# Keeping split weights in DRAM as halves, and moving subtractions and additions of squares to GpSimd

## The chip, the cores and the metric

The kernel runs on one core of a Trainium2 chip. The metric is the device time of one execution in microseconds, the median of three runs. A profile was taken of one further execution.

## The reference, cut to what matters

The program is a decoder trunk of two residual layers on one sequence of 2048 tokens with 1024 channels, all in float32.

```
xn = rms_norm(h, norm_g[layer])
even layer: z = xn @ w_in_even -> u, v, ga, xb, gb, qm, gm
  ya = chunked_sgu(u, v) * silu(ga)      # LayerNorm of v, 128x128 mixing inside chunks
  yb = multiscale_pool(xb) * silu(gb)    # trailing means of 2, 4, 8, 16 tokens, then a 128x128 map
  ym = memory_attention(qm, mem) * silu(gm)
  h  = h + concat(ya, yb, ym) @ w_out_even
odd layer: z = xn @ w_in_odd -> qc, kc, vc, gc, da, db, gd, qm, gm
  yc = swa_sink_attention(qc, kc, vc) * silu(gc)   # window of 128
  yd = conformer_conv(da, db) * silu(gd)           # 31 taps per channel, LayerNorm, swish, 512x512 map
  ym = memory_attention(qm, mem) * silu(gm)
  h  = h + concat(yc, yd, ym) @ w_out_odd
```

## The kernel before, in words

The tokens are cut into four blocks of 512 (`TB`), and each block passes through an even and an odd stage, eight stages in the order E0, E1, O0, E2, O1, E3, O2, O3 (`order`, line 921). In the trace the stages begin at about 0, 253, 453, 745, 955, 1210, 1433 and 1695 us.

**Matrix products in halves.** Every factor is split into a high half (a cast to the reduced type fp32r on ScalarE, `hi_of`, line 119) and a low half (the float32 value minus the high half, `lo_of`, line 122). A product is three matmuls (`mm3`, lines 126 to 128): high by high, high by low, low by high.

**Weights.** `wslot` (line 137) brings in one slot of 128 x 1024 floats (512 KB): one load into the buffer `wr` (two of these), the cast into `wh` on ScalarE, and the subtraction into `wl` on GpSimd or VectorE. There are four `wh` and four `wl`. In even stages each third subtraction goes to VectorE, in odd stages all go to GpSimd (`share`). An even stage uses 35 slots: 20 units of the input projection (`w_cm`), 10 of the output projection (`w_o`), 4 for v (`w_v`), and one half as large for the pool map (`bw`). An odd stage uses 38: 24, 10, 2 for keys and values (`w_kvc`) and 2 for the map behind the convolution (`dpw`). Eight more are used once for the memory (`wkv`). Each of the four blocks loads and splits its layer's slots anew.

**Work around the weights.** `proj` is one unit of input projection, 24 matmuls of 512 columns. `gate` turns a unit into a gate path. `finish` (line 330) splits a finished branch of 128 x 512 into `yh` and `yl`; there are ten of these in each stage. `out_steps` runs an output projection in eight steps, each of which ends with the addition of the result to a residual row on VectorE (line 521, `row`). `Norm` loads the next stage's input, squares it on ScalarE and adds up the squares on VectorE (`square_sum`, line 160, `p`); `split` (line 482) makes the next stage's input halves `xnh` and `xnl`, eight of each. `pace` ties the subtractions of `split`, three at a time, behind the row additions of a stage's last output projection.

**Order.** A planner in the compiler of the kernel orders each engine's instructions by a simulated timeline; the order is fixed before the run, so it changes when the engine of an instruction changes. All transfers are issued by SyncE's queue, in that order. In an odd stage the 31 taps of the convolution (line 689) are fed to VectorE two at a time after each projection (`pump`), and the events of the attention are written out by hand in `_SEQ`.

Of the kernel before, what the change touches and what calls it, by code (L numbers as in the profile page):

```python
# [10 lines left out]
F32 = mybir.dt.float32  # L11
F32R = mybir.dt.float32r
AF = mybir.ActivationFunctionType
ALU = mybir.AluOpType
# [4 lines left out]
P = 128  # L19
S = 2048  # L20
D = 1024
TB = 512
# [30 lines left out]
def trunk(ctx: ExitStack, tc: tile.TileContext, x, mem, par, par1, wkv, w_v, w_cm0, w_kvc, w_cm1, w_o0, w_o1, awt, bw, dpw, abse, out):  # L53
# [68 lines left out]
    def lo_of(eng, lo, raw, hi):  # L122
        eng.tensor_tensor(lo, raw, hi.bitcast(F32), op=ALU.subtract)  # L123
# [10 lines left out]

    turns, share = [0], [3]

    def wslot(src, n=1024, eng=None):
        raw = rp.tile([P, 1024], F32, tag="wr", name="wr", bufs=2)[:, :n]
        hi = wp.tile([P, 1024], F32R, tag="wh", name="wh", bufs=4)[:, :n]
        lo = wp.tile([P, 1024], F32R, tag="wl", name="wl", bufs=4)[:, :n]  # L140
        nc.sync.dma_start(raw, src)
        hi_of(hi, raw)
        turns[0] += 1
        lo_of(eng or (V if turns[0] % share[0] == 0 else G), lo, raw, hi)
        return hi, lo

    def view(pair, pat, **kw):
        return [t.rearrange(pat, **kw) for t in pair]
# [11 lines left out]
    def square_sum(srcs, n_buf=1):  # L160
        bufs = []
        for _ in range((n_buf + 2) // 2):
            t = p_tile().rearrange("p a b -> p (a b)")
            bufs += [t[:, :TB], t[:, TB:]]
        total, bufs = bufs[0], bufs[1:]
        for i, src in enumerate(srcs):
            sq = bufs[i % n_buf] if i else total
            A.activation(sq, src, AF.Square)
            if i:
                V.tensor_tensor(total, total, sq, op=ALU.add)  # L170
        return total, bufs[0]

    def token_scale(sums, width):
# [146 lines left out]
                bg.pop(0)()  # L320

    def proj(xn, w_cm, unit):
        wh, wl = view(wslot(w_cm[unit]), "p (k c) -> p k c", k=KC)
        pb = mm_bank()
        for k in range(KC):
            mm3(pb, wh[:, k, :], wl[:, k, :], xn[0][:, k, :], xn[1][:, k, :], k == 0, k == KC - 1)
        pump(2)
        return pb

    def finish(y):  # L330
        hi = half("yh", 4, F32R)
        lo = half("yl", 4, F32R)
        done[0] = hi_of(hi, y)
        lo_of(V, lo, y, hi)
        return hi, lo

    def gate(st, w_cm, unit):
# [113 lines left out]
    class Norm:  # L451
# [30 lines left out]
        def split(self):  # L482
            flush()
            xn = xn_tile()

            def one(k):
                hi_of(xn[0][:, k, :], self.xs[k])
                lo_of(V, xn[1][:, k, :], self.xs[k], xn[0][:, k, :])
            rate[0] = 3
            paced.extend(lambda k=k: one(k) for k in range(KC))  # L490
            return xn
# [12 lines left out]
    def out_steps(st, first, ys):  # L504
        rows = st["rows"]
        w_o = w_o1 if st["odd"] else w_o0
        n = len(ys)
        per = KC // n
        ws = {}

        def step(u):
            q, c = divmod(u, per)
            if q not in ws:
                ws[q] = view(wslot(w_o[first + q]), "p (u k n) -> p u k n", u=per, k=n)
            wh, wl = ws[q]
            pb = mm_bank()
            for k in range(n):
                mm3(pb, wh[:, c, k, :], wl[:, c, k, :], ys[k][0], ys[k][1], k == 0, k == n - 1)
            pump(2)
            row = rows[u // 2][:, (u % 2) * TB:(u % 2 + 1) * TB]  # L520
            add = V.tensor_tensor(row, pb, row, op=ALU.add)  # L521
            pace(add)

        return [lambda u=u: step(u) for u in range(KC)]
# [74 lines left out]
    def even(st, ahead):  # L599
        b, xn = st["b"], st["xn"]  # L600
        if b:
            t, wt, abias = sgu_tile()
            nc.sync.dma_start(t, sgu_d)
        xhs = [half("xc", 4) for _ in range(NT)]
        for hf in range(2):
            if b == 0 and hf == 0:
                ws = first_v
            else:
                with behind(ET.DVE):
                    ws = [view(wslot(w_v[hf, j]), "p (k n) -> p k n", k=4) for j in range(2)]  # L610
            for tt in range(NT):
                pb = mm_bank()[:, :256]
                ts = slice(tt * P, (tt + 1) * P)
                for k in range(KC):
                    wh, wl = ws[k // 4]
                    mm3(pb, xn[0][:, k, ts], xn[1][:, k, ts], wh[:, k % 4, :], wl[:, k % 4, :], k == 0, k == KC - 1)
                A.copy(xhs[tt][:, hf * 256:(hf + 1) * 256], pb)
                if hf:
                    standard(xhs[tt], xhs[tt])
        if b == 0:  # L620
            with behind(ET.PE, ET.SP, ET.Pool, ET.DVE, ET.Activation):
                wt, abias = prep_even()
                prep_odd()
            mx, total = mem_start()
            diag = token_scale(total, 256)
        q = queries(st, w_cm0, (16, 17), 4, "qm")
        if b == 0:
            memt = mem_norm(mx, diag)
        gm = [gate(st, w_cm0, 18 + n) for n in range(2)]
        if b == 0:  # L630
            prep_mem(memt)
        start_rows(st, x[b])
        hx = st["hx"] = sb.tile([P, 4, HALO + TB], F32, tag="hx", name="hx", bufs=1)
        V.tensor_copy(hx[:, :, :HALO], xtail)
        df = [None] * 4
        ym = memory(0, q, gm, lambda tt: pool_windows(st, df, tt))
        nx = ahead()
        wb = view(wslot(bw, TB), "p (g d) -> p g d", g=4)
        yb = [pool_map(st, g, df[g], wb) for g in range(3)]
        project_out(st, 8, ym)  # L640
        yb.append(pool_map(st, 3, df[3], wb))
        ya = [sgu(st, 0, xhs, wt, abias)]
        steps = out_steps(st, 4, yb)
        for f in steps[:4]:
            f()
        with behind(ET.PE):
            nx.measure()
        for f in steps[4:]:
            f()
        nx.scale()  # L650
        rate[0] = 4
        for n in range(1, 4):
            ya.append(sgu(st, n, xhs, wt, abias))
        st["next"] = nx.split()
        project_out(st, 0, ya)
        flush()
        store_rows(st, h1[b])
# [33 lines left out]

    def keys(st):
        xn, kt, va = st["xn"], st["kt"], st["va"]
        ws = [view(wslot(w_kvc[q]), "p (k n) -> p k n", k=4) for q in range(2)]
        for tt in range(NT):
            pb = mm_bank()
            ts = slice(tt * P, (tt + 1) * P)
            for k in range(KC):
                wh, wl = ws[k // 4]
                mm3(pb[:, :256], xn[0][:, k, ts], xn[1][:, k, ts], wh[:, k % 4, :], wl[:, k % 4, :],  # L700
                    k == 0, k == KC - 1)
            pump(2)
            ss = small("kss", 2)
            sq = short()
            for h in range(2):
                A.activation(sq[:, h * 64:h * 64 + 64], pb[:, h * 64:h * 64 + 64], AF.Square, accum_out=ss[:, h:h + 1])
            A.copy(va[:, 1 + tt, :], pb[:, P:2 * P])
            r = rsq("krs", ss, 2, 1.0 / 64)
            kn = sb.tile([P, P], F32, tag="kn", name="kn", bufs=2)
            for h in range(2):  # L710
                V.scalar_tensor_tensor(kn[:, h * 64:h * 64 + 64], pb[:, h * 64:h * 64 + 64], r[:, h:h + 1], gk,
                                       op0=ALU.mult, op1=ALU.mult)
            tb = tr_bank()
            T.transpose(tb[:, :P], kn, ident)
            stack_keys(kt[:, :, P + tt * P:P + (tt + 1) * P], tb[:, :P])
        V.tensor_copy(ktail, kt[:, :, TB:].bitcast(F32))
        V.tensor_copy(vtail, va[:, NT, :])
# [188 lines left out]
        return hd  # L906

    def conv_mix(st, hd, ys):
        ws = [view(wslot(dpw[q]), "p (k n) -> p k n", k=2) for q in range(2)]
        for u in range(4):  # L910
            pb = mm_bank()
            for k in range(4):
                us = slice(u * P, (u + 1) * P)
                wh, wl = ws[k // 2]
                mm3(pb, wh[:, k % 2, us], wl[:, k % 2, us], hd[k][0], hd[k][1], k == 0, k == 3)
            pace(V.scalar_tensor_tensor(ys[u], pb, 0.25, ys[u], op0=ALU.mult, op1=ALU.mult))
        return [finish(y) for y in ys]
# [3 lines left out]
    order = [(0, 0), (0, 1), (1, 0), (0, 2), (1, 1), (0, 3), (1, 2), (1, 3)][:_STAGES]  # L921
    lead = Norm(x[0], par_of("ng0"), False, 3)
    nc.sync.dma_start(pc, par)
    first_v = [wslot(w_v[0, 0], eng=G)]
    lead.measure()
    with behind(ET.DVE):
        first_v.append(wslot(w_v[0, 1], eng=V))
    first_v = [view(w, "p (k n) -> p k n", k=4) for w in first_v]
    xn = lead.scale_split()
    for n, (is_odd, b) in enumerate(order):  # L930
# [114 lines left out]
```

## Time and profile before

| what | value |
|---|---|
| median of three runs | 1969.15 us (1968.65 to 1969.47) |
| the profiled execution's own time | 1970.85 us |
| its span, from the first to the last instruction | 1968.9 us |
| busy in the span: TensorE, weight loads | 96%, 80% |
| busy in the span: VectorE, ScalarE, GpSimd | 70%, 42%, 44% |
| moved by transfers | 218.96 MB, 111 GB/s on average |

An engine's share says how much of the span it had an instruction in flight. Matmuls overlap each other, so 96% for TensorE says how little of the span it was without work, not that each instant was full. What a change can save is in the places where TensorE waits, and these are read from its idle times with what ended them.

### The profile page before, as it was taken

To read this page: it belongs to the slowest core of one execution; us is meant where nothing else is said; L and a number is where in the kernel's file an instruction comes from. 1 tells how busy PE (TensorE), PEld (TensorE's weight loads), DVE (VectorE), ACT (ScalarE), POOL (GpSimd) and SP (SyncE) were. 2 spreads that over 40 slices of the span, in tenths; PEclk is the share of its full clock that TensorE was granted. 3 is DMA by queue.
4 is the path that set the end of the run, shared out by engine and by line. 5 is a ranking of instruction groups with operands and counts; after the bars stand their busy time and mean duration, and the time that the engine had idled before them with its cause. 6 is when DMAs were issued, how large, how long until landed. Compare 5 with 4: busy or idle time off the path is not lost.

```text
span 1968.9 us, 26523 instructions
## 1 busy us (share of the span) xinstructions
PE 1899.1 (96%) x10034; PEld 1569.0 (80%) x10034; DVE 1374.2 (70%) x2262; ACT 825.3 (42%) x1663; POOL 872.8 (44%) x593
## 2 busy tenths in 40 slices
PE   6999999999998999999999899999999989999999
PEld 6878888787886878878788687988878767888687
DVE  6776544645999673565699967355569986699954
ACT  4453324423355442442435443353333544435532
POOL 3672225323555443623445443453245544445542
PEclk9999999999999999999999999999999999999999
DMA  5443353334322334232532233432252223532122
GB/s 207 152 137 113 102 173 106 109 99 166 97 86 70 103 107 160 96 113 86 177 97 67 68 124 132 136 113 97 86 178 86 75 66 111 166 108 71 59 76 75
DMA packets 61440, 218.96 MB, mean 111 GB/s; under 512 B 6785, under 2 KB 6913, under 8 KB 61185
## 3 DMA queue, kind: packets, MB, share of 16 engines
q1 hardware_dynamic: 61312, 217.27, 33.9%
q8 instruction: 79, 1.29, 0.3%
q14 instruction: 49, 0.39, 0.1%
HBM read 198.63 MB, written 18.61 MB: 110 GB/s over the span
## 4 chain that ended last, share of the span: by engine, by line
PE 47%; DVE 9%; ACT 1%; issue 0%; DMA 0%; POOL 0%; ACTq 0%; POOLq 0%; SPq 0%
PE mm L126 12%; PE mm L127 12%; PE mm L128 12%; DVE cv L689 3%; PE cv L128 2%; PE cv L126 2%; PE cv L127 2%; DVE xnl L123 1%; PE pv L417 1%; PE tr L385 1%; PE tr L312 1%; PE tr L313 1%; DVE row L521 1%; PE pv L357 1%; DVE pt L853 1%; DVE q L123 0%
## 5 line engine op out<-in xcount | busy, mean ns | idle before, releaser
L123 POOL TENSOR_TENSOR wl<-wr,wh 128x1024 fp32r<-128x1024 f32 (+1 forms) x250 | 606.6, 2428 | 866.6 <-ACT wh L120 808.2
L120 ACT CAST wh<-wr 128x1024 fp32r<-128x1024 f32 (+1 forms) x300 | 312.6, 1042 | 655.0 <-PE mm L127 358.6
L126 PE MATMUL mm<-xnh,wh 128*128 128x512 f32 x1176 | 464.3, 395 | 0.4 <-ACT u L354 0.4
L128 PE MATMUL mm<-xnh,wl 128*128 128x512 f32 x1176 | 461.6, 393 | 0.2 <-DVE wl L123 0.2
L127 PE MATMUL mm<-xnl,wh 128*128 128x512 f32 x1176 | 460.7, 392 | 0.0
L689 DVE SCALAR_TENSOR_TENSOR cv<-hx,dwh,cv 128x512 f32<-128x512 f32 x464 | 349.0, 752 | 9.1
L128 PEld LDWEIGHTS mm<-xnh,wl 128*128 128x128 f32 x1176 | 221.3, 188 | 47.2 <-issue 1.2
L127 PEld LDWEIGHTS mm<-xnl,wh 128*128 128x128 f32 x1176 | 221.6, 188 | 45.9 <-issue 2.8
L126 PEld LDWEIGHTS mm<-xnh,wh 128*128 128x128 f32 x1176 | 221.4, 188 | 44.0 <-issue 0.6
L126 PE MATMUL mm<-yh,wh 128*128 128x512 f32 x534 | 215.5, 406 | 23.8 <-DVE row L521 14.4
L127 PE MATMUL mm<-yl,wh 128*128 128x512 f32 x534 | 210.6, 394 | 1.1 <-DVE yl L123 1.1
L128 PE MATMUL mm<-yh,wl 128*128 128x512 f32 x534 | 210.5, 394 | 0.0
L521 DVE TENSOR_TENSOR row<-mm,row 128x512 f32<-128x512 f32 x160 | 109.1, 686 | 122.9 <-PE mm L128 122.6
L126 PEld LDWEIGHTS mm<-yh,wh 128*128 128x128 f32 x534 | 100.9, 190 | 56.3 <-DVE row L521 23.1
L127 PEld LDWEIGHTS mm<-yl,wh 128*128 128x128 f32 x534 | 101.0, 189 | 21.6 <-DVE yl L123 2.0
L128 PEld LDWEIGHTS mm<-yh,wl 128*128 128x128 f32 x534 | 100.9, 189 | 21.4 <-issue 0.2
L123 DVE TENSOR_TENSOR wl<-wr,wh 128x1024 fp32r<-128x1024 f32 (+1 forms) x50 | 66.3, 1326 | 68.8 <-ACT wh L120 68.7
L403 ACT ACTIVATE p<-tr,mnb,qm 128x256 f32<-128x256 f32 x128 | 70.6, 561 | 69.6 <-DVE mnb L400 65.1
L377 POOL TENSOR_SCALAR p<-p,mrd 128x256 f32<-128x256 f32 x128 | 64.1, 521 | 79.5 <-DVE mrd L406 78.4
L126 PE MATMUL mm<-wh,xnh 128*128 128x256 f32 x320 | 91.8, 287 | 2.9 <-ACT xnh L120 1.8
L128 PE MATMUL mm<-wh,xnl 128*128 128x256 f32 x320 | 91.0, 285 | 1.3 <-DVE xnl L123 1.1
L126 PE MATMUL cv<-xnh,wh 128*128 128x512 f32 x232 | 92.1, 397 | 0.0
(226 smaller groups left out, 3378.3 us busy)
## 6 DMA issues: line engine op xcount, KB each, us to landing
wr<-in_w_cm_dram SPq DMA_DIRECT2D x176, 512.0 KB, 3.5
wr<-in_w_o_dram SPq DMA_DIRECT2D x80, 512.0 KB, 3.5
wr<-in_w_v_dram SPq DMA_DIRECT2D x16, 512.0 KB, 3.5
row<-in_x_dram SPq DMA_DIRECT2D x16, 512.0 KB, 4.1
h<-row SPq DMA_DIRECT2D x16, 512.0 KB, 3.5
row<-h SPq DMA_DIRECT2D x16, 512.0 KB, 3.9
out_dram<-row SPq DMA_DIRECT2D x15, 512.0 KB, 2.7
x<-in_x_dram SPq DMA_DIRECT2D x8, 512.0 KB, 3.6
```

Of the source, the lines that this page charges most:

```text
L120: return A.copy(hi, raw)
L123: eng.tensor_tensor(lo, raw, hi.bitcast(F32), op=ALU.subtract)
L126: T.matmul(out, lhsT=lh, rhs=rh, start=first, stop=False)
L127: T.matmul(out, lhsT=lh, rhs=rl, start=False, stop=False)
L128: T.matmul(out, lhsT=ll, rhs=rh, start=False, stop=last)
L312: T.matmul(out, lhsT=q[g][:, cols], rhs=keys[:, g], start=True, stop=False)
L313: T.matmul(out, lhsT=q[g][:, cols], rhs=keys[:, 2 + g], start=False, stop=True)
L357: T.matmul(sp[:, 2 * tt:2 * tt + 2], lhsT=sq[:, tt * P:(tt + 1) * P], rhs=par_of("bones"), start=True, stop=True)
L377: G.tensor_scalar(p[:, h, :], p[:, h, :], rd[:, h:h + 1], 1.0, op0=ALU.mult, op1=ALU.mult)
L403: A.activation(p[:, h, :], banks[h // 2][:, (h % 2) * 256:(h % 2) * 256 + 256], AF.Exp, bias=nb[:, h:h + 1], scale=qr[:, tt, h:h + 1], acc ...
L521: add = V.tensor_tensor(row, pb, row, op=ALU.add)
L689: V.scalar_tensor_tensor(dst, src, w, acc, op0=ALU.mult, op1=ALU.add)
```

## The change

Three things change. A slot of weights is now one buffer of two halves (`w`, 128 x 2 x 1024, four of them, as many bytes as the four `wh` and four `wl`). At its first use it is loaded and split as before and then written to DRAM as halves (1 MB); at each later use the 1 MB of halves is loaded straight into the buffer, with no cast and no subtraction. The eight slots of the memory have no key and stay as they were. The low halves of the branches (`finish`) and of the next stage's input (`split`) are computed on GpSimd in place of VectorE. The additions of squares in `square_sum` go to GpSimd too, but for the very first norm, which has three buffers.

```diff
-    def wslot(src, n=1024, eng=None):
+    halves = {}
+
+    def wslot(src, n=1024, eng=None, key=None):
+        w = wp.tile([P, 2, 1024], F32R, tag="w", name="w", bufs=4)[:, :, :n]
+        hi, lo = w[:, 0], w[:, 1]
+        if key in halves:
+            nc.sync.dma_start(w.bitcast(F32), halves[key])
+            return hi, lo
         raw = rp.tile([P, 1024], F32, tag="wr", name="wr", bufs=2)[:, :n]
-        hi = wp.tile([P, 1024], F32R, tag="wh", name="wh", bufs=4)[:, :n]
-        lo = wp.tile([P, 1024], F32R, tag="wl", name="wl", bufs=4)[:, :n]
         nc.sync.dma_start(raw, src)
         hi_of(hi, raw)
         turns[0] += 1
         lo_of(eng or (V if turns[0] % share[0] == 0 else G), lo, raw, hi)
+        if key:
+            halves[key] = tc.dram_tile([P, 2, n], F32, name="w_" + "_".join(map(str, key)))
+            nc.sync.dma_start(halves[key], w.bitcast(F32))
         return hi, lo
...
             if i:
-                V.tensor_tensor(total, total, sq, op=ALU.add)
+                (V if n_buf > 1 else G).tensor_tensor(total, total, sq, op=ALU.add)
...
         done[0] = hi_of(hi, y)
-        lo_of(V, lo, y, hi)
+        lo_of(G, lo, y, hi)
...
                 hi_of(xn[0][:, k, :], self.xs[k])
-                lo_of(V, xn[1][:, k, :], self.xs[k], xn[0][:, k, :])
+                lo_of(G, xn[1][:, k, :], self.xs[k], xn[0][:, k, :])
```

Every call of `wslot` but that for `wkv` now passes a key that names its matrix and slot.

## Rows read from the trace of the kernel before

**Rows 1.** The page: span, and busy time of each engine.

```profile
span 1968.9 us, 26523 instructions
PE 1899.1 (96%) x10034; PEld 1569.0 (80%) x10034; DVE 1374.2 (70%) x2262; ACT 825.3 (42%) x1663; POOL 872.8 (44%) x593
```

**Rows 2.** What TensorE waited for: total us, times, longest us.

```profile
PE mm L126 <- DVE row L521: 15.7, 17, 1.6
PE tr L179 <- DVE p L170: 11.1, 1, 11.1
PE mm L126 <- ACT yh L120: 8.5, 4, 3.9
PE pv L862 <- DVE pt L853: 5.0, 3, 2.3
```

**Rows 3.** Timelines at a stage's end: start, us, what, [idle before <- releaser].

```profile
254.24 0.50 PE L126 MATMUL cv<-yh,wh 128*128 128x512 f32 x1 [1.52 <-DVE row L521]
...
945.95 4.09 DVE L123 TENSOR_TENSOR xnl<-x,xnh 128x512 fp32r<-128x512 f32 x3
949.96 0.68 DVE L521 TENSOR_TENSOR row<-mm,row 128x512 f32<-128x512 f32 x1
...
946.74 2.75 POOL L123 TENSOR_TENSOR wl<-wr,wh 128x1024 fp32r<-128x1024 f32 x1 [5.06 <-ACT wh L120]
...
1699.51 0.50 PE L126 MATMUL mm<-yh,wh 128*128 128x512 f32 x1 [1.00 <-DVE row L521]
```

**Rows 4.** Stretches of O1: us, busy us (instructions) of PE, PEld, DVE, ACT, POOL, PEclk, transfers.

```profile
985.00:995.00 10.00, 10.00 (x46) 8.29 (x45) 9.10 (x14) 3.22 (x5) 3.21 (x2) 1.00 0.37 107
...
1095.00:1105.00 10.00, 7.68 (x40) 5.45 (x39) 9.77 (x19) 6.97 (x21) 5.88 (x6) 1.00 0.16 52
1115.00:1125.00 10.00, 6.09 (x22) 4.66 (x19) 9.91 (x22) 7.14 (x21) 3.00 (x5) 0.66 0.17 53
```

**Rows 5.** Groups by line and shape: busy us, mean ns | idle before.

```profile
L123 POOL TENSOR_TENSOR wl<-wr,wh 128x1024 fp32r<-128x1024 f32 x248 | 604.0, 2437 | 857.5 <-ACT wh L120 799.1 <-PE mm L128 24.3 <-ACT pt L387 11.8
L120 ACT CAST wh<-wr 128x1024 fp32r<-128x1024 f32 x296 | 310.1, 1048 | 651.2 <-PE mm L127 358.6 <-issue 110.2 <-PE cv L127 66.7
L123 DVE TENSOR_TENSOR yl<-gt,yh 128x512 fp32r<-128x512 f32 x80 | 66.3, 845 | 12.3 <-ACT yh L120 12.3
L170 DVE TENSOR_TENSOR p<-p 128x512 f32<-128x512 f32 x59 | 54.0, 916 | 26.3 <-ACT p L168 25.0
L841 POOL TENSOR_TENSOR p<-p,crd 128x512 f32<-128x512 f32 x32 | 32.7, 1042 | 7.9 <-DVE crd L838 7.9
```

**Rows 6.** Durations ns min/median/max of single lines, first and last start.

```profile
L123 POOL TENSOR_TENSOR wl<-wr,wh x250: 1292/2402/3143, 11.1 to 1944.9; 128x1024 fp32r<-128x1024 f32 x123, 128x512 fp32r<-128x512 f32 x2
L123 DVE TENSOR_TENSOR yl<-gt,yh x80: 675/686/2546, 149.3 to 1944.3; 128x512 fp32r<-128x512 f32 x80
L123 DVE TENSOR_TENSOR xnl<-x,xnh x28: 674/685/2891, 249.5 to 1691.3; 128x512 fp32r<-128x512 f32 x28
L677 DVE COPY htail<-hx x16: 167/945/2060, 506.4 to 1826.8; 128x30 f32<-128x30 f32 x16
```

**Rows 7.** Transfers: a load of weights, a larger one, the busiest stretch.

```profile
wr<-in_w_cm_dram SPq DMA_DIRECT2D x176, 512.0 KB, 3.5
...
sgu<-sgu_d SPq DMA_DIRECT2D x3, 768.0 KB, 4.3
...
2.00:8.00 6.00, 0.00 (x0) 0.00 (x0) 2.15 (x4) 3.39 (x7) 0.00 (x0) 1.00 0.95 370
```

**Rows 8.** E0 and O0 by engine, as rows 4; last are transfer share, GB/s.

```profile
0.00:253.00 253.00, 234.47 (x1330) 197.67 (x1330) 163.97 (x233) 107.31 (x178) 116.11 (x86) 1.00 0.42 140
...
453.00:745.00 292.00, 280.94 (x1416) 227.99 (x1415) 233.35 (x407) 130.89 (x288) 131.25 (x87) 0.99 0.33 108
```

**Rows 9.** What ScalarE's squares waited for: total us, times, longest us.

```profile
ACT p L168 <- DMA x<-h: 16.4, 7, 3.8
...
ACT p L168 <- DMA x<-in_x_dram: 10.2, 6, 2.5
```

More of the change, by code (lines that the diff above doesn't have):

```diff
@@ L322, in proj @@
     def proj(xn, w_cm, unit):
-        wh, wl = view(wslot(w_cm[unit]), "p (k c) -> p k c", k=KC)
+        wh, wl = view(wslot(w_cm[unit], key=("cm", int(w_cm is w_cm1), unit)), "p (k c) -> p k c", k=KC)
         pb = mm_bank()
@@ L513, in step @@
             if q not in ws:
-                ws[q] = view(wslot(w_o[first + q]), "p (u k n) -> p u k n", u=per, k=n)
+                ws[q] = view(wslot(w_o[first + q], key=("o", int(st["odd"]), first + q)), "p (u k n) -> p u k n", u=per, k=n)
             wh, wl = ws[q]
@@ L609, in even @@
                 with behind(ET.DVE):
-                    ws = [view(wslot(w_v[hf, j]), "p (k n) -> p k n", k=4) for j in range(2)]
+                    ws = [view(wslot(w_v[hf, j], key=("v", hf, j)), "p (k n) -> p k n", k=4) for j in range(2)]
             for tt in range(NT):
@@ L637, in even @@
         nx = ahead()
-        wb = view(wslot(bw, TB), "p (g d) -> p g d", g=4)
+        wb = view(wslot(bw, TB, key=("bw",)), "p (g d) -> p g d", g=4)
         yb = [pool_map(st, g, df[g], wb) for g in range(3)]
@@ L693, in keys @@
         xn, kt, va = st["xn"], st["kt"], st["va"]
-        ws = [view(wslot(w_kvc[q]), "p (k n) -> p k n", k=4) for q in range(2)]
+        ws = [view(wslot(w_kvc[q], key=("kvc", q)), "p (k n) -> p k n", k=4) for q in range(2)]
         for tt in range(NT):
@@ L908, in conv_mix @@
     def conv_mix(st, hd, ys):
-        ws = [view(wslot(dpw[q]), "p (k n) -> p k n", k=2) for q in range(2)]
+        ws = [view(wslot(dpw[q], key=("dpw", q)), "p (k n) -> p k n", k=2) for q in range(2)]
         for u in range(4):
@@ L923, in trunk @@
     nc.sync.dma_start(pc, par)
-    first_v = [wslot(w_v[0, 0], eng=G)]
+    first_v = [wslot(w_v[0, 0], eng=G, key=("v", 0, 0))]
     lead.measure()
     with behind(ET.DVE):
-        first_v.append(wslot(w_v[0, 1], eng=V))
+        first_v.append(wslot(w_v[0, 1], eng=V, key=("v", 0, 1)))
     first_v = [view(w, "p (k n) -> p k n", k=4) for w in first_v]
```

## The prediction

> **What bounds the kernel now.** I read the page first, then what TensorE waited for, then the timelines at those waits. TensorE has an instruction in flight for 1899.1 of 1968.9 us [rows 1], so 69.8 us of idle time, and what it loses at a lower clock, is all that a change off TensorE can win; the number of matmuls stays. Of the 69.8 us the start takes about 16: one wait of 11.1 us for the first norm [rows 2] and two smaller ones behind it, none of which the change touches. The largest other releaser is the row addition, 15.7 us in 17 waits, then the branches' high halves with 8.5 us and the masked copy in the attention, `pt`, with 5.0 us [rows 2].
>
> Two places hold these. At a stage's end TensorE waits for a row addition because VectorE is making the next input's low halves: three `xnl` took 4.09 us from 945.95, and the row addition behind them began only at 949.96 [rows 3]. Alone, one takes 0.685 us (the median); the longest took 2.891 us [rows 6]. GpSimd began a `wl` of 2.75 us at 946.74, inside that stretch [rows 3]. Ten such waits lie between 254.24 and 1699.51, at six of the seven changes of stage, 12.1 us together; the first was 1.52 us, the last 1.00 us [rows 3]. In the middle of an odd stage VectorE itself is full: 9.77 and 9.91 of 10 us, with TensorE at 7.68 and 6.09, and in the second stretch the granted clock averaged 0.66 of its 2.4 GHz level, after TensorE had stood idle [rows 4].
>
> **Part 1, the weights.** Of 300 splits, 292 slots have a key, 73 in each of four passes; so 219 splits go and 81 stay. ScalarE loses 219 casts of 1.048 us, 230 us [rows 5]; its 42% share [rows 1] sits off the path, so I count nothing. GpSimd loses about 183 subtractions of 2.437 us, 446 us, and VectorE about 36; all of these leave E1, O1 and later stages, and E0 and O0 keep theirs. TensorE hardly waited for a `wl`, so the direct gain is nothing; the indirect one is that a two-input operation on VectorE no longer waits for a GpSimd one (above).
>
> Transfers grow. The 219 later loads are twice as long: 114 MB more. The 73 stores add 76 MB. That makes 409 MB in place of 219, 208 GB/s over the span. E0 gets some 36 MB of stores on top of 140 GB/s, so 283 GB/s; O0 some 40 MB on top of 108, so 244 GB/s [rows 8]. The busiest stretch shows 370 GB/s at a transfer share of 0.95 [rows 7], so both means fit. One slot of halves, by the rows of 512 and 768 KB (3.5 and 4.3 us [rows 7]), should land in about 5 us. Its cover is three other slots; in a stretch of projections 46 matmuls take 10 us [rows 4], 0.22 us each, so a slot of 24 lasts 5.2 us and three of them 16. Where two slots are held (keys and values, the convolution's map) the cover is one to two slots, still over 5 us. A store waits in SyncE's queue for the subtraction, and the next raw load is queued behind it; but that load wants the buffer which the same subtraction frees. So stores cost 0. If the cover were gone, one landing of 5 us at each of eight stage starts would cost 40.
>
> The loads of the next input (`x`) queue on the same engines. ScalarE's squares waited 26.6 us for them in 13 waits [rows 9]; behind one more slot each (1.05 MB at 370 GB/s, 2.8 us) that grows by 36 us. ScalarE's queue holds whatever comes next: casts of branches, tanh of gates. It has slack nearly everywhere, so I take 2 us, with 0 and 36 as ends.
>
> **Part 2, low halves to GpSimd.** Eighty `yl` and 56 `xnl` leave VectorE. On GpSimd no subtraction of 512 columns at this place is shown: the bounds are 1.042 us (the product at line 841 [rows 5]) and 1.29 us (the shortest `wl`, the half-size form [rows 6]). I take 1.29, the same operation. GpSimd's load becomes 873 - 446 + 136 x 1.29 + 55 for the squares, about 655 us of the span: not a bound.
>
> At the stage's end the eight casts are done on ScalarE before the row additions begin, so eight `xnl` in a row (10 us) run beside a projection of 21 us (96 matmuls), free of the row additions. Of the 12.1 us I take 11; the ends are 0 and 12.1. The Trainium skill's page "SBUF — State Buffer", section "Who interferes with whom", says that a VectorE instruction with two SBUF inputs is held for the whole of a GpSimd instruction that reads SBUF; the 2.891 us against 0.685 [rows 6] agrees. A row addition has one input in PSUM, and by that page GpSimd would not hold it.
>
> In the middle of an odd stage VectorE loses four `yl` (2.7 us at 0.686 us [rows 6]) and the time held by `wl`: the copy at line 677 took 0.945 us (median) against 0.167 (least) [rows 6], 3.1 us a stage for four of them. That is some 6 us per odd stage, 24 in four. What can be won there is at most 8.5 + 5.0 us of waits [rows 2] and 3.4 us of clock (0.34 of 10 us [rows 4]) per odd stage if each loses as much, 27 us. The planner's order decides how much arrives: I take half of the 24, 12 us; ends 0 and 27.
>
> Against this stands latency. Where four branches finish together before their output projection (once per odd stage), the fourth `yl` comes 4 x (1.29 - 0.69) = 2.4 us later, 9.6 us in four stages; I take half, 5 us, since each product's first matmul needs `yh` alone. At the last projection of all eight stages one `yl` is 0.6 us late, 5 us; I take 3, since three other branches cover 2 us of it; if all 24 output projections paid, 14 us.
>
> **Part 3, the squares.** Fifty-two additions of 0.916 us [rows 5] leave VectorE and cost about 1.05 us on GpSimd (the same row 841). A chain of seven grows by 1 to 3 us; in the timelines most norms finish over 10 us before their use, one of them about 5 us, so 0. If nothing covered it, seven norms would pay 3 us each, 21.
>
> **The sum.** 11 + 12 - 5 - 3 - 2 = 13 us gained. Against the profiled execution's own 1970.85 us (span 1968.9 and 1.95 around it) that makes 1957.85; that execution stands 1.7 above the median, so the forecast is 1956 us (1969.15 - 13).
>
> **The rivals.**
>
> *Odd stages unblocked.* VectorE's relief arrives whole: 12.1 + 27 - 5 gives 34 us, 1935 us. For it: VectorE at 98% where TensorE idles [rows 4]. Against it: the taps are put between other instructions by a fixed order, and that is not changed by a shorter queue. Chance 0.15.
>
> *Latency on GpSimd eats the gain.* GpSimd pays 1.29 where VectorE alone pays 0.69. If all 24 projections pay 0.6 (14 us) and four joint finishes the full remaining 1.8 (7 us), 21 of the 23 us won are gone: 1967 to 1969 us. For it: `yl` is the second matmul of each product. Against it: TensorE waited 1.1 us in all for `yl` before, so it had slack. The Trainium skill's "GPSIMD Engine Reference", section "Engine selection", says to keep elementwise work on VectorE, GpSimd being about twice as slow with two inputs; the 1.29 against 0.69 agrees, and by that rule alone the moves lose time. Chance 0.17.
>
> *Late inputs (slower).* With 1.05 MB per slot in the queue, `x` lands 2.8 us later, ScalarE stands, and branches behind it come late. There are 14 pairs of late loads (two per norm, seven norms). If ten reach TensorE, 28 us are lost and 13 won: 1984 us. It decides from five of the 14 upward. For it: the waits exist already [rows 9]. Against it: ScalarE gains 230 us of slack, and the means stay below 370 GB/s. Stalled first uses in E0 and O0 would look alike. Chance 0.18.
>
> **How the numbers follow.** The forecast's case (1944 to 1965 us) has chance 0.50. Ranges: 1925 to 1944 for the first rival, 1965 to 1972 for the second, 1973 to 1996 for the third. Holding eight in ten, I leave out the far part of the first and of the third: 1934 to 1974 us; the forecast's own range is 1944 to 1965. What this measurement can tell from no change is 0.2%, 1965.2 to 1973.1 us. Faster: 0.50 + 0.15 + a little of the second, 0.69. Same: 0.14. Slower: 0.17.
>
> **What would show it.** Right: no row addition behind `xnl` at a stage's end, and the row-addition waits down from 15.7 to about 5 us; GpSimd near 655 us, VectorE near 1160, ScalarE near 600; no TensorE wait on a `w` transfer. Wrong: new waits of TensorE for `yl` or `xnl` on GpSimd, for `w` loads, or ScalarE's squares waiting far over 26.6 us for `x`. A plan that places the taps or the attention in another order could move either sign by several us, and no row of before shows it.

## The result and the profile after

The kernel with the change takes 1940.46 us (median of four runs, 1939.18 to 1942.02) where the kernel before took 1968.90 in the same comparison: a ratio of 0.9851, interval 0.9839 to 0.9863. That is 28.4 us won. The forecast said 1956 (13 us won), with 1934 to 1974 as its range. The sign and the range held; the size was less than half of what came, and the experiments show that the largest term stood in the wrong part. The time lies below the forecast's own case (1944 to 1965) and in what the first rival named.

The page of the changed kernel, which answers to [rows 1], and its transfers:

```profile
span 1940.0 us, 26058 instructions
PE 1893.4 (98%) x10034; PEld 1570.8 (81%) x10034; DVE 1109.8 (57%) x2039; ACT 614.7 (32%) x1444; POOL 661.5 (34%) x597
...
DMA packets 72460, 409.00 MB, mean 211 GB/s; under 512 B 7952, under 2 KB 8080, under 8 KB 35344
...
w<-w_cm SPq DMA_DIRECT2D x132, 1024.0 KB, 4.9
```

TensorE's idle time fell from 69.8 us to 46.6 (1940.0 - 1893.4). That is 23.2 of the 28.9 us by which the span shrank; the other 5.7 are TensorE's busy time, for the same 10034 matmuls. A row after a wait shows why some of a wait counts as busy: the matmul that starts again is drawn with 0.50 us where one in the stream has 0.39. With 34 waits in place of 55 that is some 2 us; where the rest of the 5.7 went was not traced.

What TensorE waits for now, as [rows 2]:

```profile
PE tr L187 <- DVE p L178: 11.2, 1, 11.2
PE mm L126 <- ACT yh L120: 10.6, 4, 3.2
PE mm L126 <- DVE row L529: 2.5, 5, 1.2
...
PE cv L126 <- DMA w<-w_v: 2.3, 1, 2.3
PE mm L127 <- POOL yl L123: 2.1, 2, 1.5
```

The row additions (now line 529) went from 15.7 us and 17 waits to 2.5 us and 5. The masked copy `pt` is gone from the list. The start is as before, and the branches' high halves took 10.6 us in place of 8.5. Of the new waits the two largest are near 2 us: one transfer of halves that came late, and `yl` from GpSimd (VectorE's `yl` had cost 1.1).

VectorE and GpSimd at the end of E2, as [rows 3]:

```profile
934.60 0.69 DVE L529 TENSOR_TENSOR row<-cv,row 128x512 f32<-128x512 f32 x1 [6.56 <-PE cv L128]
935.21 1.28 DVE L529 TENSOR_TENSOR row<-mm,row 128x512 f32<-128x512 f32 x2
...
930.08 5.05 POOL L123 TENSOR_TENSOR xnl<-x,xnh 128x512 fp32r<-128x512 f32 x4
935.08 5.04 POOL L123 TENSOR_TENSOR xnl<-p,xnh 128x512 fp32r<-128x512 f32 x4
```

The eight `xnl` run in 10 us on GpSimd beside the row additions, which no longer stand behind them. Read alone, this looks like the moved work paying off. The experiments below say otherwise.

The middle of O1 and the first passes E0 and O0, as [rows 4, 8]:

```profile
1085.00:1095.00 10.00, 10.00 (x62) 8.22 (x58) 9.77 (x19) 2.12 (x4) 2.99 (x4) 1.00 0.37 114
1095.00:1105.00 10.00, 6.17 (x25) 4.02 (x25) 9.21 (x21) 6.75 (x21) 5.99 (x8) 0.76 0.22 93
0.00:250.00 250.00, 231.73 (x1320) 196.86 (x1321) 143.06 (x211) 105.93 (x176) 141.68 (x108) 1.00 0.80 286
450.00:735.00 285.00, 276.36 (x1403) 225.08 (x1402) 199.03 (x370) 127.80 (x285) 169.41 (x119) 0.99 0.71 250
```

One of the two short stretches of O1 is full now, the other is as empty as before, at a granted clock of 0.76. The first passes move 286 and 250 GB/s (forecast 283 and 244). By the last row addition of each stage E0 ends at 264.2 us (266.1 before) and O0 takes 268.1 us (265.1 before, and 265.3 in the run e1 below, which has the same transfers).

### The profile page after: what moved, and what is told of

Read it like the earlier page. It is cut to its first block, busy times and chain, and to the rows that moved or that the text cites. A ratio compares the mean times of both kernels' runs of the same rounds, so it can differ in the third digit from the quotient of the medians.

```text
span 1940.0 us, 26058 instructions
## 1 busy us (share of the span) xinstructions
PE 1893.4 (98%) x10034; PEld 1570.8 (81%) x10034; DVE 1109.8 (57%) x2039; ACT 614.7 (32%) x1444; POOL 661.5 (34%) x597
## 4 chain that ended last, share of the span: by engine, by line
PE 88%; DVE 4%; DMA 2%; ACT 2%; POOL 2%; issue 1%; SPq 0%; POOLq 0%; ACTq 0%; DVEq 0%
PE mm L126 22%; PE mm L128 21%; PE mm L127 21%; PE cv L128 4%; PE cv L126 4%; PE cv L127 4%; PE pv L425 2%; PE tr L320 1%; PE tr L393 1%; DVE cv L697 1%; PE tr L321 1%; POOL w L123 1%; PE pv L365 1%; PE pv L870 1%; PE pv L592 1%
## 5 line engine op out<-in xcount | busy, mean ns | idle before, releaser
L126 PE MATMUL mm<-xnh,w 128*128 128x512 f32 x1176 | 463.1, 394 | 1.0 <-ACT u L362 0.9
L128 PE MATMUL mm<-xnh,w 128*128 128x512 f32 x1176 | 460.0, 391 | 0.0
L127 PE MATMUL mm<-xnl,w 128*128 128x512 f32 x1176 | 459.1, 390 | 0.0
L128 PEld LDWEIGHTS mm<-xnh,w 128*128 128x128 f32 x1176 | 220.7, 188 | 46.4 <-issue 1.0
L126 PEld LDWEIGHTS mm<-xnh,w 128*128 128x128 f32 x1176 | 220.9, 188 | 44.9 <-ACT u L362 1.4
L127 PEld LDWEIGHTS mm<-xnl,w 128*128 128x128 f32 x1176 | 221.0, 188 | 43.3 <-issue 0.2
L126 PE MATMUL mm<-yh,w 128*128 128x512 f32 x534 | 215.5, 406 | 13.1 <-ACT yh L120 10.6
L127 PE MATMUL mm<-yl,w 128*128 128x512 f32 x534 | 211.6, 396 | 2.1 <-POOL yl L123 2.1
L128 PE MATMUL mm<-yh,w 128*128 128x512 f32 x534 | 210.9, 395 | 0.0
L123 POOL TENSOR_TENSOR w<-wr,w 128x1024 fp32r<-128x1024 f32 x66 | 158.9, 2410 | 121.8 <-ACT w L120 108.8
L123 POOL TENSOR_TENSOR yl<-gt,yh 128x512 fp32r<-128x512 f32 x80 | 102.6, 1297 | 253.7 <-ACT yh L120 253.6
L126 PEld LDWEIGHTS mm<-yh,w 128*128 128x128 f32 x534 | 101.7, 191 | 42.1 <-ACT yh L120 14.1
L127 PEld LDWEIGHTS mm<-yl,w 128*128 128x128 f32 x534 | 101.8, 191 | 24.5 <-POOL yl L123 3.0
L128 PEld LDWEIGHTS mm<-yh,w 128*128 128x128 f32 x534 | 101.3, 190 | 21.2
```

The costliest lines, as they stand in the source:

```text
L126: T.matmul(out, lhsT=lh, rhs=rh, start=first, stop=False)
L127: T.matmul(out, lhsT=lh, rhs=rl, start=False, stop=False)
L128: T.matmul(out, lhsT=ll, rhs=rh, start=False, stop=last)
```

## The experiments

Each kernel ran against the kernel before on the same chip. "Reuse" is the part of the change that keeps the halves in DRAM. The control k0 splits the weights in each pass, as before, in the changed code; k1, k2 and k4 leave a part of that work out, and their result is another. A plan is the order that the planner gives each engine; each edit gets its own.

| kernel | median us | ratio to before (95%) |
|---|---|---|
| the whole change | 1940.46 | 0.9851 (0.9839 to 0.9863) |
| e1 reuse alone | 1935.78 | 0.9818 (0.9804 to 0.9833) |
| e2 the moves alone | 1998.42 | 1.0130 (1.0112 to 1.0148) |
| e3 reuse + input's low halves on GpSimd | 1934.10 | 0.9812 (0.9796 to 0.9829) |
| e4 reuse + branches' low halves on GpSimd | 1939.52 | 0.9838 (0.9822 to 0.9855) |
| e5 reuse + squares on GpSimd | 1936.29 | 0.9835 (0.9818 to 0.9851) |
| h1 whole change without the branches' move | 1937.18 | 0.9832 (0.9817 to 0.9847) |
| f1 reuse, GpSimd's load put back | 1989.52 | 1.0102 (1.0074 to 1.0130) |
| f8 the same, on the slot before | 1988.51 | 1.0098 (1.0068 to 1.0129) |
| f2 reuse, ScalarE's load put back | 1951.72 | 0.9914 (0.9899 to 0.9929) |
| f9 the same, on the slot before | 1956.12 | 0.9929 (0.9911 to 0.9947) |
| f4 reuse, 114 MB more traffic | 1938.55 | 0.9842 (0.9828 to 0.9857) |
| g1 reuse, another order of the scores | 1936.22 | 0.9835 (0.9820 to 0.9850) |
| k0 control: split in each pass, one buffer | 1971.24 | 1.0005 (0.9993 to 1.0017) |
| k1 control without the subtractions | 1945.68 | 0.9884 (0.9868 to 0.9900) |
| k2 control without the casts | 1973.64 | 1.0024 (1.0014 to 1.0035) |
| k4 control without VectorE's third | 1967.04 | 0.9992 (0.9982 to 1.0002) |

**The parts one by one.** After the result I held a theory A: the gain comes mostly from GpSimd's weight subtractions leaving the later stages, and partly from the moved work. Its rivals: B, the moved work does it all; C, the weights do it all and the moves are neutral or cost.

```diff
 e1: finish, split and square_sum as before, reuse as in the change
-    lo_of(G, lo, y, hi)                                  # finish
+    lo_of(V, lo, y, hi)
...
-    lo_of(G, xn[1][:, k, :], self.xs[k], xn[0][:, k, :]) # split
+    lo_of(V, xn[1][:, k, :], self.xs[k], xn[0][:, k, :])
...
-    (V if n_buf > 1 else G).tensor_tensor(total, total, sq, op=ALU.add)
+    V.tensor_tensor(total, total, sq, op=ALU.add)
 e2: the three on G, and in wslot
+    key = None
 e3: split on G, e4: finish on G, e5: squares on G, the other two on V
```

> The reuse of split weights alone; branches, input and squares stay on VectorE as before. Theory A (mine now): the wins come mostly from GpSimd's weight subtractions leaving the later stages, because two-input VectorE operations no longer stand behind them, and partly from the moved work: 1945 to 1953 us, row-addition waits of TensorE 4 to 9 us in place of 17.6. Rival B (the moved work does it all, the weights bring nothing): 1963 to 1972 us, row-addition waits near 17. Rival C (the weights do it all and the moves are neutral or cost): 1936 to 1943 us.

> Branches, input and squares on GpSimd, but every pass splits its weights anew, as before. Theory A: the stage ends gain, but GpSimd carries about 1100 us and its low halves stand behind weight subtractions: 1953 to 1964 us, with new TensorE waits for yl on GpSimd of 3 to 10 us. Rival B: 1938 to 1945 us. Rival C: 1966 to 1980 us.

> Weights reused and the next input's low halves on GpSimd; branches and squares on VectorE. Theory A: the stage ends are then free, 4 to 8 us better than the weights alone, row-addition waits under 4 us. Rival C: within 2 us of the weights alone.

> Weights reused and the branches' low halves on GpSimd; the next input's and the squares on VectorE. Theory A: 1 to 5 us better than the weights alone, from VectorE in the middle of odd stages. The forecast's latency term (8 us of cost) would make it 0 to 8 us worse than the weights alone.

> Weights reused and only the additions of squares on GpSimd. If the cost of the three moves is a sum of small latencies (reuse alone to the whole change: about 5 us), the squares cost 0 to 2 us over reuse alone: ratio to the kernel before 0.981 to 0.984. If the squares' longer chain (GpSimd 1.36 us an addition) is the cost, they alone cost 4 us or more: 0.984 or above.

Reuse alone takes 1935.78 us, 34 us less than before and less than the whole change. The moves alone take 1998.42, 28 us more than before. Rival C holds, 0.2 us past the fast edge of what it named for e1 and 18 us past the slow edge of what it named for e2. The page of e1:

```profile
PE 1889.7 (98%) x10034; PEld 1569.6 (81%) x10034; DVE 1231.6 (64%) x2227; ACT 614.8 (32%) x1444; POOL 422.6 (22%) x409
```

and TensorE's waits (engine, operation and line that waited, what it waited for; total us, count, longest):

```profile
PE mm L126 <- ACT yh L120: 10.6, 4, 3.2
PE mm L126 <- DVE row L529: 5.9, 8, 1.5
...
PE mm L127 <- DVE yl L123: 0.6, 1, 0.6
```

The row-addition waits fell from 15.7 to 5.9 us although `xnl` is still on VectorE. In e1's timeline the waits behind `xnl` remain at one stage end, before O0 (1.51 and 1.43 us at 464.5 and 469.0), where weights are still being split; at the ends before O1 and O2 there are none. For the moves alone:

```profile
PE 1912.3 (96%) x10034; PEld 1577.7 (79%) x10034; DVE 1237.2 (62%) x2074; ACT 824.9 (41%) x1663; POOL 1105.5 (55%) x781
```

and TensorE's waits:

```profile
PE tr L723 <- DVE kn L720: 21.6, 9, 5.9
...
PE mm L127 <- POOL yl L123: 8.4, 7, 1.5
```

GpSimd now has 1105.5 us of work. The largest wait is for the keys (`kn`): they need a small power from GpSimd (line 166, 0.7 us) and ahead of it `krsa`, a VectorE operation on two columns. At one such wait (4.6 us, until 497.04) the two engines show this:

```profile
490.79 4.88 POOL L123 TENSOR_TENSOR w<-wr,w 128x1024 fp32r<-128x1024 f32 x2 [7.74 <-ACT w L120]
493.71 1.99 DVE L164 TENSOR_SCALAR krsa<-kss 128x2 f32<-128x2 f32 x1 [6.25 <-ACT u L715]
```

The next `krsa`, at 496.90, takes 0.16 us. This one took 1.99, until GpSimd's two weight subtractions were over, and the power began at 495.77. VectorE at 62% did not help.

On top of reuse, the input's halves change nothing that can be measured (0.9812 against 0.9818), and the squares little if anything (0.9835; the interval overlaps). The branches were tried from the other side too:

```diff
 h1: the whole change but
-        lo_of(G, lo, y, hi)
+        lo_of(V, lo, y, hi)
```

> The whole change, but the branches' low halves stay on VectorE. If the branches on GpSimd are what the whole change loses against reuse alone: 1932 to 1937 us, and no TensorE wait for yl over 1 us in all. If the three moves lose by their sum: 1938 to 1942 us.

h1 takes 1937.18 us, at the edge of what was expected if the branches are the cost; 2.6 us of `yl` waits remained, now on VectorE, so the wait list does not bear that expectation out. e4 against e1 and the whole against h1 both say that the branches on GpSimd cost some 3 to 4 us; each pair's intervals overlap, and the two agree.

**Is it GpSimd's load or ScalarE's?** In f1 and f2 each later load of halves is followed by an operation that nobody reads; in f8 and f9 it works on the slot before, to keep it from waiting for the transfer.

```diff
 f1, after the load of halves (f8: on the halves of the slot before)
+    turns[0] += 1
+    if turns[0] % share[0]:
+        d = rp.tile([P, 1024], F32, tag="wr", name="wr", bufs=2)[:, :n]
+        G.tensor_tensor(d, hi.bitcast(F32), lo.bitcast(F32), op=ALU.subtract)
 f2, after each load (f9: on the slot before)
+    A.copy(d, hi.bitcast(F32))
```

> Reuse alone, but after each load of halves GpSimd makes a subtraction of both halves (128x1024) into a buffer that nobody reads, as often as it made one before. GpSimd's load is back, off every chain but the slot's release. Theory A (GpSimd's instruction holds two-input VectorE work and stands ahead of small GpSimd work): 15 to 28 of the 34 us are lost again, 1950 to 1964 us, with row-addition waits over 12 us. Rival D (the casts that left ScalarE): under 4 us lost. Rival E (another order by the planner): nothing lost, or a loss with row-addition waits still near 6.

> Reuse alone, but after each load of halves ScalarE copies the high half (128x1024) into a buffer that nobody reads: ScalarE's 230 us are back. Theory A: at most 5 us lost. Rival D: 12 us or more lost, with longer TensorE waits for yh and for gates.

> Reuse alone, with GpSimd's 182 or so subtractions of 128x1024 put back on the halves of the slot loaded one earlier, which have landed by then; nobody reads the result. It differs from the earlier run with the load put back in that GpSimd's queue no longer stands for a transfer. Theory A (what left GpSimd is most of the win): 1950 to 1970 us, GpSimd's idle time for transfers under 150 us in place of 670, row-addition waits over 10 us. If that earlier loss came from GpSimd standing for transfers alone: 1934 to 1942 us.

> Reuse alone, with ScalarE's 219 copies of 128x1024 put back on the slot loaded one earlier. Theory A: 1935 to 1940 us, the earlier loss of 16 us being ScalarE standing for transfers. Theory A plus D (ScalarE's load counts too): 1943 to 1953 us, with TensorE waits for the queries (q) and the keys (kn) as long as in that run, 11 us together.

Putting GpSimd's load back costs 53 us, more than reuse had won; ScalarE's 16 to 20. Both miss what theory A named, and ScalarE's loss is of the size that rival D (the casts) named; k2 below speaks against D. f8 and f9 failed in their purpose: GpSimd's idle time before these operations is still 656 us for transfers in f8, and in f9 ScalarE's is 539, so both loads may cost more here than they did before, and the sizes are no clean shares of the win. The page of f8 shows one thing cleanly:

```profile
PE 1913.3 (96%) x10034; PEld 1578.7 (79%) x10034; DVE 1325.5 (66%) x2227; ACT 616.5 (31%) x1444; POOL 870.2 (44%) x593
```

and TensorE's waits:

```profile
PE tr L729 <- DVE kn L726: 12.7, 7, 3.8
...
PE mm L126 <- DVE row L536: 11.3, 12, 2.5
...
PE mm L126 <- DVE gt L357: 9.7, 5, 3.4
```

VectorE has the same 2227 instructions as in e1, and its busy time rose from 1231.6 to 1325.5 us. Nothing was added to VectorE; the 94 us came with GpSimd's operations, and I read them as time that it stood, as `krsa` did above.

**Taking one part away from the old structure.** These four kernels load the raw slot in every pass, as before.

```diff
 k0: as before, but both halves in one buffer
 k1, from the second pass on (the high half is used twice, no low half)
+    if again:
+        return hi, hi
 k2, from the second pass on (a sum of the raw slot in place of the halves)
+    if again:
+        e.tensor_tensor(lo, raw, raw, op=ALU.add)
+        return lo, lo
 k4, from the second pass on (VectorE's third has the high half twice)
+    if again and e is V:
+        return hi, hi
```

> The control: every pass loads and splits its weights as before, branches, input and squares on VectorE as before; only the two halves lie in one buffer. All theories of load say 1965 to 1973 us, as before. Rival E (another plan or the one buffer brought the win): under 1955 us.

> As the control, but from the second pass on the low half is not computed: the matmuls take the high half in its place, so loads and casts stay and some 183 subtractions on GpSimd and 36 on VectorE go (the result is another). Theory A (the subtractions held VectorE and stood ahead of GpSimd's small work): 20 to 30 us won, 1938 to 1950 us. If the two engines' loads count alike: 10 to 18 us won.

> As the control, but from the second pass on the cast on ScalarE is not made: GpSimd or VectorE adds the raw slot to itself in place of the subtraction, and the matmuls take that for both halves (the result is another). Subtraction-like work stays, ScalarE's 230 us go. Theory A: at most 10 us won. By the copies put back on ScalarE (16 to 20 us lost): 10 to 20 us won.

> As the control, but from the second pass on only those subtractions are left out that VectorE made (36, each third in even stages); the matmuls take the high half there (the result is another). Theory A: 0 to 4 us won, in the even stages alone. If VectorE's own share of the weights is the even stages' loss (4 to 6 us a stage against reuse alone): 8 to 14 us won.

The control is as before (1.0005), so neither the one buffer nor the control's plan brought the win. Without the casts nothing is won (1.0024, a loss at the bound of what can be told). Without VectorE's third 2 to 4 us at most. Without the subtractions 0.9884, 23 us won (25.6 against the control's median), at full casts and 219 MB of traffic; by k4 VectorE's own third is at most 2 to 4 of it, which leaves some 20 for GpSimd's. The page of k1 and, behind it, that of the control:

```profile
PE 1893.7 (98%) x10034; PEld 1569.2 (81%) x10034; DVE 1232.1 (63%) x2227; ACT 826.5 (43%) x1663; POOL 422.4 (22%) x409
```

and TensorE's waits:

```profile
PE mm L126 <- DVE row L528: 5.3, 7, 1.6
```

```profile
PE 1898.3 (97%) x10034; PEld 1565.1 (80%) x10034; DVE 1364.1 (69%) x2262; ACT 824.8 (42%) x1663; POOL 871.0 (44%) x593
```

and TensorE's waits:

```profile
PE mm L126 <- DVE row L526: 16.6, 18, 1.6
```

Between the last row additions of O0 and of E2 TensorE waits for nothing in k1 and in e1, where it waited 5.4 us in the kernel before and 6.3 in the control, most of it for row additions. That a slot is ready sooner is not the reason: for a low half of the weights TensorE had waited 0.7 us in the control.

E1 can be taken to start with the first matmul of its `v`; in each of these kernels 1378 matmuls stand ahead of it. (The 253 us given at the top for this stage lies inside E0's last output projection.) The lines are of the kernel before, the control, k1 and e1:

```profile
265.25 0.28 PE L126 MATMUL mm<-wh,xnh 128*128 128x256 f32 x1
...
271.80 0.28 PE L126 MATMUL mm<-w,xnh 128*128 128x256 f32 x1
...
269.87 0.28 PE L126 MATMUL mm<-w,xnh 128*128 128x256 f32 x1
...
263.72 0.28 PE L126 MATMUL mm<-w,xnh 128*128 128x256 f32 x1
```

From there to the end of the span the kernel before takes 1703.6 us (1968.9 - 265.3), the control 1692.6 (1964.4 - 271.8), k1 1672.2 (1942.1 - 269.9) and e1 1671.5 (1935.2 - 263.7). So where the subtractions are gone, k1 and e1 are alike, 20 us shorter than the control, and the casts that went and the traffic that came need no share there. The 6 us by which e1 is ahead of k1 lie in E0, in which both split every weight. k1 leaves out the same subtractions as e1, so it is not these; TensorE idles 3.5 us less in e1 up to that point. Which difference of plan, or which store, does it I did not settle.

**Traffic, and an attempt at more.**

```diff
 f4, after each load of halves
+    d = rp.tile([P, 1024], F32, tag="wr", name="wr", bufs=2)[:, :n]
+    nc.sync.dma_start(d, src)
 g1, in the odd stage's order of events (reuse alone otherwise)
-    ... V2 f2 s0 V3 f2 e s1 o2 v0 ...
+    ... V2 f2 V3 f2 e s0 o1 s1 o1 v0 ...
```

> Reuse alone, and behind each load of halves one more load of the raw slot (512 KB) into a buffer that nobody reads: 114 MB more, some 520 MB in all, 270 GB/s. If traffic is hidden (my forecast's part 1): under 3 us lost. If late inputs are near to deciding (the forecast's third rival): 10 us or more lost, with ScalarE's squares waiting over 60 us for x.

> Reuse alone, with the first memory scores of an odd stage (s0) traced behind the end of the window attention (e) in place of ahead of it, so that ScalarE's four exponentials don't stand ahead of the four yh casts. Theory: the yh wait of TensorE (10.6 us in four stages) falls under 4 us and 4 to 10 us are won over reuse alone. Rival: TensorE waits as long for the scores' chain (maximum, exponentials, turning): within 2 us of reuse alone.

f4 moved 523 MB at 270 GB/s and took 1938.55 us, 0.9842 against e1's 0.9818: 3 us by the medians, 5 by the ratios, between the two expectations, with intervals that overlap. ScalarE's squares waited 22.4 and 16.3 us for `x`, 39 in all, not over 60. So late inputs, the forecast's third rival, are not near to deciding at 211 GB/s.

In g1 the waits for `yh` fell only from 10.6 to 6.3 us, and other waits grew (`yl` 2.4, the gates' `u` 2.5). 1936.22 us: the rival held, nothing was won.

The fastest versions beat both kernels: reuse alone, and reuse with the input's halves on GpSimd, at 0.9818 and 0.9812 of before, against 0.9851 for the whole change.

## Why the prediction was right or wrong

**Where TensorE waits: right.** The row additions behind `xnl` and the middle of the odd stages were the places. Row additions (of both tiles, 17.6 to 2.5 us) and `pt` (5.0 to nothing) make up most of the 23.2 us of idle time that went. The signs that the prediction named for being right came true too (row-addition waits, the engines' loads), but e1 shows the first of them without the moves: it told the place, not the cause.

**Part 1, the step that failed.** The sum has no gain for the weights at all. The prediction said of the weights that "the direct gain is nothing" and named an indirect one, that VectorE no longer waits for a GpSimd operation; then it booked the 11 us of the stage ends under Part 2, as the fruit of moving `xnl`, and sized the held time of VectorE at 3.1 us per odd stage. Both were wrong. k1 and e1 win 23 and 34 us with `xnl` where it was. The term that was mis-sized is VectorE's held time: put at 12 us over four stages (3.1 each) beside 2.7 each for `yl`, and booked as the moves' gain, it measures 94 us in f8 against e1. From before to e1 VectorE's busy time fell by 142.6 us (1374.2 to 1231.6), of which its own weight subtractions explain about 46 (66.3 to 19.7 and one half-size form), so some 96 were standing time. From the control to k1 the same working gives 87 (1364.1 to 1232.1, less 45), and the span past the start of E1 fell by 20 us there: most of the time that VectorE stands does not reach the end. It is spread over many lines, as these groups of the kernel before show, then the same of e1, and one of the control:

```profile
L123 DVE TENSOR_TENSOR km<-u,km 64x512 fp32r<-64x512 f32 x32 | 42.5, 1328 | 2.9 <-ACT km L300 2.2
...
L123 DVE TENSOR_TENSOR xnl<-x,xnh 128x512 fp32r<-128x512 f32 x28 | 35.5, 1308 | 0.0
...
L592 DVE TENSOR_TENSOR gt<-u,gt 128x512 f32<-128x512 f32 x16 | 25.2, 1574 | 0.5
...
L677 DVE COPY htail<-hx 128x30 f32<-128x30 f32 x16 | 15.4, 965 | 0.1
```

```profile
L123 DVE TENSOR_TENSOR km<-u,km 64x512 fp32r<-64x512 f32 x32 | 27.7, 865 | 22.7 <-ACT km L308 22.5
...
L123 DVE TENSOR_TENSOR xnl<-x,xnh 128x512 fp32r<-128x512 f32 x28 | 22.2, 835 | 0.0
...
L600 DVE TENSOR_TENSOR gt<-u,gt 128x512 f32<-128x512 f32 x16 | 11.0, 690 | 0.4
...
L685 DVE COPY htail<-hx 128x30 f32<-128x30 f32 x16 | 3.9, 242 | 0.1
```

```profile
L597 DVE TENSOR_TENSOR gt<-u,gt 128x512 f32<-128x512 f32 x16 | 11.1, 691 | 0.4
```

A copy of 30 columns fell from 0.965 to 0.242 us, `km` from 1.328 to 0.865, `xnl` itself from a mean of 1.308 to 0.835. The product `gt` in the even stages fell from 1.574 to 0.690, but it has 0.691 in the control too, which is as slow as before: which lines stand depends on the plan. The sum depends on it less. Added up over all VectorE instructions, the time above the least of the same line is 229 us in the kernel before, 221 in the control and 223 in f8, but 121 in k1 and in e1. The prediction had the least and the longest durations of such lines in front of it and used one of them. The sum over all lines, 229 us, would have been an upper bound; 121 us of it are still there when the subtractions of the later passes are gone.

The rule of the Trainium skill that it leaned on ("SBUF — State Buffer", section "Who interferes with whom") agrees with this in kind: `xnl` has two SBUF inputs, and that page says that such an instruction is held for the whole of a GpSimd instruction that reads SBUF; copies stand among those that, by that section, can take the pair of ports shared with GpSimd under conditions. No run here tests the ports themselves.

**ScalarE's 230 us off the path: right where tested.** k2, the casts gone alone, wins nothing. f2 and f9 lose 16 to 20 us when copies come back, but these stand behind transfers, so they do not refute it. After the start of E1, k1 with the casts and e1 without them are alike.

**Part 2, the moves: wrong in sign.** The prediction gave them 11 + 12 - 5 - 3 = 15 us, most of it relief of VectorE. On top of reuse they cost: 0.9851 for all three against 0.9818, intervals just apart, 5 us by the medians and 6 by the ratios. The price of the operation was right (1.297 us measured for `yl` and `xnl`, forecast 1.29), and the latency term too in kind: 8 us were booked for the branches, 3 to 4 measured. What was not there was the gain; reuse alone had already taken most of the row-addition waits away. Without reuse the moves lose 28 us, on a GpSimd of 1105.5 us. The second rival, latency on GpSimd eating the gain, is right about the moves; it missed that the gain lay elsewhere. The first rival, VectorE's relief arriving whole, has the time in its range (1925 to 1944) and not the cause: it counted the moves as a gain, 12.1 us at the stage ends among it. That the stated range held is luck to that extent, since a gain of 34 us that was not booked and a loss of about 6 met in it. The "GPSIMD Engine Reference" of the Trainium skill, section "Engine selection", said to keep such work on VectorE; e1 against the whole change and e2 agree, and e3, with the input's halves moved alone, shows no cost.

**Part 3, the squares: cost 0 held within the interval.** An addition took 1.358 us on GpSimd where 1.05 was forecast.

**Traffic: right.** 409 MB, 211 GB/s, 4.9 us for a slot of halves (forecast 409, 208, 5; 7.0 for the twelve of `w_v`), one late load of 2.3 us, and squares that waited 25.0 us for `x` (15.4 and 9.6) where 26.6 had been [rows 9].

**Engine loads: right.** GpSimd 661.5 us (forecast 655), ScalarE 614.7 (600), VectorE 1109.8 (1160; the difference is standing time).

**The sum.** 13 us were forecast and 28.4 came: reuse gave 34 where nothing but the 2 us of late inputs was booked, as a loss, and the moves took about 6 where 15 net were booked to them.

**Still open.** How the 23 us of k1 divide between VectorE held by GpSimd and GpSimd's own small operations queued behind a subtraction (both show in f8: 94 us of VectorE, and 12.7 us of waits for `kn`); and the 6 us by which e1 and the whole change begin E1 earlier than k1. Each kernel has its own plan, so a few us of any single difference may be the plan's.

## What to carry to other kernels

When one edit takes work off an engine and another moves work off the engine that it was holding up, price them in both orders: here the first alone won more than both. An engine's mean duration far above its least, in many lines at once, can be time that another engine takes from it; sum that excess, as an upper bound, before counting what moving work away would free. Off-path engines are not free of cost: GpSimd at 44%, with some 2 us of TensorE's waits on it by name, still set some 20 us of the end.

## What the runs showed of the hardware

VectorE was busy 94 us longer for the same 2227 instructions when GpSimd had 448 us more of two-input work (f8 against e1), some 0.2 us for each us of it; a VectorE operation on two columns took 1.99 us beside two GpSimd subtractions and 0.16 us behind them (e2). TensorE's waits cost more than their listed idle time: the idle time fell by 23.2 us and the span by 28.9 at the same number of matmuls. Nearly doubling the traffic to 409 MB, at 0.80 of the transfer engines' time in E0, delayed one load that TensorE noticed, by 2.3 us, and none in e1.
